# A later place for woven products, and two output weights that stay, in a two-layer streaming encoder

## The chip, the cores and the metric

The program runs on one core of one Trainium2 chip. The metric is device time in microseconds of one execution. TensorE multiplies, VectorE, ScalarE and GpSimd do the rest, and SyncE (SP) issues nearly all DMAs. Each engine works through its own instruction list in order: an instruction that waits holds up all behind it on that engine.

## What is computed

One step of a small encoder for 1024 prompt frames and 32 sample frames (1056 columns), model width 1024, all in float32. Layer 0 is an mLSTM mixer (8 heads, chunks of 64 frames, a recurrence from chunk to chunk), layer 1 a sliding-window attention of 16 query heads over two shared key/value heads. A SwiGLU feed-forward (width 2816) follows each, and every part ends in a LayerNorm of `alpha * x + part(x)`.

```
x = layer_norm(ALPHA * x + mix, ln_g[layer, 0], ln_b[layer, 0])
x = layer_norm(ALPHA * x + swiglu(x, w_gu[layer], w_down[layer]), ln_g[layer, 1], ln_b[layer, 1])
```

For layer 1, `mix` is `o.reshape(B, T, D_ATT) @ w_out`, with `o` the attention's output; this last product with `w_out` (in the kernel `wout_b`) is one of the two places of the change.

## The kernel before

**Products.** Every large product is made of three float32r matmuls per 128 rows (high times high, high times low, low times high: lines 677, 678, 679 in `gemm`). Columns are cut in three groups of 384, 384 and 288 for projections, and in four quarters of 264 for output tiles, LayerNorms and the feed-forward. An output tile (`out_tile`) is 24 matmuls: 8 row blocks of a weight times 3, and a weight comes in two halves of 512 KB each (`f` 0 and 1), the split float32r form that is stored in DRAM after its first use (`wout_b<-w`, `wout_b<-area`) and loaded again later (`w<-wout_b`, line 425).

**Weights.** `Weights` runs a fixed list of units, each with two halves as jobs. A half takes one of five buffers `w` (SLOTS) until `W.done`, or a place of its own (`W.home`) where one is set. Raw weights (`wr<-in_gu` and the like) come by line 372.

**Weaving.** The main program writes out the weight products; small tasks (mLSTM chunks, attention, LayerNorms) are generators that say with `At(engine, reads, ...)` what they wait for next. A planner in the kernel (`Clock`) keeps due times of all tiles while the program is written. After each three matmuls of `gemm`, `Weave.tick` takes tasks whose step is due by `now + LEAD`; `now` is the planner's TensorE time, and for TensorE's steps LEAD is -0.2 us, so they are written only when their operands are due 0.2 us ago or earlier. `Weave.until` and `drain` step the earliest task whatever its due time, with no lead, until a condition holds; the main program uses them where it needs a result.

**mLSTM (70 to 302 us).** Each of 36 chunk items has on TensorE: the score product L1216, the key transpose L1218, the value products L1239 and L1241, the state product L1243, and at last the transposes L1305 of the result `ht`, with VectorE, ScalarE and GpSimd work between.

**Attention (1200 to 1447 us).** 72 items, each of two score products (L2049, L2050) per head, softmax work, transposes L2068 into a tile `T`, a cast to `hi` (L2074, ScalarE) and a subtraction to `lo` (L2078, VectorE), then the value products L2084 (`hi`) and L2085 (`lo`) into `O`. Beside them a list PLAN of weight products runs: queries, and output tiles ("o") of quarters 0 and 1; their weights are loaded for each. At the end the attention's result is copied to SX pieces (L2117, L2119), and act is read back (L2121).

**Late quarters.** After PLAN a `Mixer` opens the area E (`ex`), and `norm_tail` runs quarters 0 to 3: for 0 and 1 the tiles are done, `late_out` only notes them; for 2 and 3 it computes 8 output tiles, m = 0 to 7. `U_OUT_B` are eight units loaded anew for this: the first two take `w` buffers, the other six have homes in E (the first half of tile 2 still takes a buffer). Each quarter's LayerNorm is a woven task: mean and variance products (L737) on TensorE, additions L921, squares L757, folds L744, and so on to SX pieces (L794, L800), which the feed-forward's products then read. The LayerNorm of a quarter starts after that of two quarters before. The first block of the feed-forward (`up_plain`) runs on two quarters, and waits for all LayerNorms before its second half.

Of the kernel before, what the change touches and what calls it, by code (L numbers as in the profile page):

```python
# [19 lines left out]
KT = D // P  # L20
# [264 lines left out]
class Weave:  # L285


    LEAD = {"PE": -0.2}

    def __init__(self, clk):  # L290
        self.clk, self.tasks = clk, []
# [12 lines left out]
    def tick(self, until=0.0):  # L304
        while True:
            now = max(self.clk.now, until)
            best = None
            for i, t in enumerate(self.tasks):
                at = self._start(t)
                if at is not None and at <= now + self.LEAD.get(self._engine(t), 0.45):  # L310
                    if best is None or at < best[0]:
# [204 lines left out]
def kernel(ctx: ExitStack, tc: tile.TileContext, A, O):  # L516
# [41 lines left out]
    def add(name, idx):  # L558
        units.append(A[name][idx] if idx is not None else A[name])
        return len(units) - 1  # L560
# [19 lines left out]
    def again(name, m):  # L580

        u = add(name, m)
        if (name, m) in split:
            halves[u] = split[name, m]
        else:
            split[name, m] = kept[u] = dram.tile([P, 2, 2, D // 2], F32, name=f"{name}_{m}")
            first[name, m] = u
        return u

    def add_ffn(layer):  # L590
        up, dn = {}, []
        for c in range(2):
            for i in range(FIRST):
                up[i, c] = [add("gu", 2 * (layer * FT + i) + k) for k in range(2)]
        for i in range(FIRST, FT):
            up[i] = add_pair("gu", 2 * (layer * FT + i))
        for b in range(TAIL):
            dn.append([add_pair("dn", 4 * (layer * TAIL + b) + 2 * j) for j in range(2)])
        dn.append([add("dnt", KT * layer + m) for m in range(KT)])
        on_vector.update((u, 1) for u in dn[TAIL])  # L600
        on_vector.update((u, 1) for i in range(FIRST) for c in range(2) for u in up[i, c])
        U_UP.append(up)
        U_DN.append(dn)
# [15 lines left out]
    U_B = {}  # L619
    for kind, m, g in PLAN:  # L620
        name, m0 = {"q": ("wqb", m), "k": ("wkv", 0), "v": ("wkv", 1), "o": ("wout_b", m)}[kind]
        U_B[kind, m, g] = again(name, m0)
    U_OUT_B = [again("wout_b", u) for u in range(8)]
    add_ffn(1)
    on_vector.update((u, 1) for u in U_OUT_A)
    on_vector.update((u, f) for u in U_Q[:1] + U_KV + [U_B['q', 0, 0]] for f in range(2))
# [5 lines left out]
    W = Weights(nc, clk, new_weight, units, pairs, on_vector, kept, halves, wv)  # L632
# [824 lines left out]
    lx = Mixer(ea.close, U_OUT_A[:6])  # L1457
# [19 lines left out]
    def out_tile(u, m, g, hold=False):  # L1477
        cols = group(g)
        t = psbank(hold)
        ps, z = t[:, :N4], ACT[:, m, cols]  # L1480
        gemm(ps, wcols(u), [(SX[:, 0, k, cols], SX[:, 1, k, cols]) for k in range(KT)])

        def out():
            yield At("DVE", [ps], [z])
            nc.vector.scalar_tensor_tensor(z, z, ALPHA, ps, op0=ALU.mult, op1=ALU.add)
            release(psx[1][0], "d", t)

        if hold:
            return wv.launch(out(), True)
        nc.vector.scalar_tensor_tensor(z, z, ALPHA, ps, op0=ALU.mult, op1=ALU.add)  # L1490
# [396 lines left out]
    eb = ExitStack()  # L1887
# [10 lines left out]
    def k_part(src, c0, n):  # L1898

        for g in range(2):  # L1900
            r = slice(64 * g, 64 * g + 64)
            o = slice(64 - 64 * g, 128 - 64 * g)
            dst = slice(c0, c0 + n)
            nc.scalar.copy(KH[g][r, dst], src[r])
            nc.vector.tensor_sub(KL[g][r, dst], src[r], KH[g][r, dst].bitcast(F32))
            nc.scalar.copy(KH[g][o, dst], KH[g][r, dst].bitcast(F32))
            nc.vector.tensor_copy(KL[g][o, dst], KL[g][r, dst].bitcast(F32))
# [16 lines left out]
    def q_group(j, g):  # L1924

        t0, n = GRP[g]
        t, ps = project(U_B["q", j, g], g, True)
        W.done(U_B["q", j, g])
        sc = -(HD ** -0.5)

        def out():
            yield At("Activation", [ps], room=[ring(pb, "Q", 4)])
            q = Q[j, g] = new(pb, "Q", [P, 2, 384], F32R, bufs=4)
            for h in range(2):
                r = slice(HD * h, HD * h + HD)
                nc.scalar.activation(q[r, h, :n], ps[r], AF.Copy, scale=sc)
            for h in range(2):
                r, o = slice(HD * h, HD * h + HD), slice(HD - HD * h, P - HD * h)
                yield At("DVE", [q[r, h, :n]])
                nc.vector.scalar_tensor_tensor(  # L1940
                    q[o, h, :n], ps[r], sc, q[r, h, :n].bitcast(F32), op0=ALU.mult, op1=ALU.subtract
                )
            release(psx[1][0], "d", t)
            ast["ready"] += 1

        wv.launch(out(), True)
# [7 lines left out]
    def v_parts(c, src, L):  # L1954

        src = src.rearrange("p (g d) -> p g d", g=2)
        nc.scalar.copy(VR[:L, c, :, 0, :], src)
        nc.vector.tensor_sub(VR[:L, c, :, 1, :], src, VR[:L, c, :, 0, :].bitcast(F32))
# [41 lines left out]
    def v_turn(group):  # L2000
        for c, c0, L, g, off in CH:
            if g == group:
                yield At("PE", [vT[g][:, off : off + L]], room=[ring(psb, "O", 2)])
                pt = new(psb, "O", [P, 512], bufs=2, hold=True)
                nc.tensor.transpose(pt[:L, :P], vT[g][:, off : off + L], ident[:])
                yield At("Activation", [pt[:L, :P]])
                src = pt[:L, :P].rearrange("p (g d) -> p g d", g=2)
                nc.scalar.copy(VR[:L, c, :, 0, :], src)
                yield At("DVE", [VR[:L, c, :, 0, :]])
                nc.vector.tensor_sub(VR[:L, c, :, 1, :], src, VR[:L, c, :, 0, :].bitcast(F32))  # L2010
                release(psb, "O", pt)
                ast["v"] = c + 1
# [119 lines left out]
    for kind, m, g in PLAN:  # L2132
        u = U_B[kind, m, g]
        if kind == "q":
            wv.until(lambda: ast["scored"] >= 3 * (done - 3))
            q_group(m, g)
            done += 1
        elif kind == "o":
            wv.until(lambda: ast["split"] > g and (not g or ast["scored"] >= min(53 + 3 * m, 72)))
            outs.append(out_tile(u, m, g, True))  # L2140
            W.done(u)
        else:
            for t in (1, 2):
                (k_group if kind == "k" else v_group)(u, t)
                if kind == "v":
                    wv.launch(v_turn(t))
            W.done(u)
            if kind == "v":
                v_parts(9, cv[:], P)
                k_part(ck, SEQ, P)  # L2150
                nc.sync.dma_start(O["p_k"], kout[:, :P])
                nc.sync.dma_start(O["s_k"], kout[:, P:])
                nc.sync.dma_start(O["p_v"], vT[2][:, 128:256])
                nc.sync.dma_start(O["s_v"], vT[2][:, 256:])
    wv.drain(task)
    wv.drain(parts)
    for t in outs:
        wv.drain(t)
    lx = Mixer(eb.close, U_OUT_B[2:])

    def late_out(g, cols, after):
        for m in range(KT):
            if g > 1:
                out_tile(U_OUT_B[m], m, g)
                if g == 3:
                    W.done(U_OUT_B[m])
            after(range(KT), m)

    tasks = norm_tail(2, late_out, [lx])
    ffn(1, 3, tasks, lx, True)  # L2170
    wv.until(lambda: not wv.tasks)
# [126 lines left out]
```

## Time and profile before

| | us |
|---|---|
| median of 3 runs | 2220.59 (2217.61 to 2221.95) |
| the profiled execution | 2219.07 |
| its span in the trace | 2217.3 |
| TensorE busy (matmul) | 2182.8 |
| VectorE, ScalarE, GpSimd busy | 1512.6, 1021.9, 800.0 |

Lines are those of the code above. A "wait" of an engine is idle time just before an instruction, with the instruction that released it; a row of the timeline has it in brackets. The chain of waits goes back from the last instruction to what released each step. T in names is a PSUM tile, `d` the PSUM tile of a weight product, `ln` that of a LayerNorm's product.

### The profile page before, as it was taken

The page shows a single profiled execution, that of the slowest core. Times are in us where ns is not written, and L with a number is a line of the kernel's source. Part 1 is how long each engine was busy: PE and PEld are TensorE (multiplying, and loading weights), DVE is VectorE, ACT ScalarE, POOL GpSimd, SP SyncE. Part 2 cuts the span into 40 slices and gives each one's busy share as a digit, 9 for nine tenths or more (in the row PEclk, how much of TensorE's full clock was granted, in tenths as well). Part 3 has the DMA queues.
Part 4 walks back from the last instruction along what each step waited for, and adds up shares of the span by engine and source line. Part 5 has one row for each costly group of instructions (what it writes and reads, how often), then busy time and mean ns, then how long its engine had stood idle before and what let it go on. Part 6 is the DMA issues. An engine that isn't in the chain of part 4 may idle for free.

```text
span 2217.3 us, 44432 instructions
## 1 busy us (share of the span) xinstructions
PE 2182.8 (98%) x17116; PEld 2150.9 (97%) x17116; DVE 1512.6 (68%) x3030; ACT 1021.9 (46%) x2308; POOL 800.0 (36%) x805
## 2 busy tenths in 40 slices
PE   9999999999999999999999999999999999999997
PEld 9989999999999999999999999989999999999997
DVE  5566566777766566476677887778675665566677
ACT  4554454555434444321245877657443443421234
POOL 1343300001544545444401565500454554544510
PEclk9999999999999999999999999999999999999999
DMA  4455522302434424598516568761344344489712
GB/s 154 143 155 174 185 81 74 118 30 77 170 123 173 148 107 165 188 309 283 174 66 223 175 194 267 233 212 58 117 166 146 128 155 145 135 290 322 244 52 78
DMA packets 218052, 356.69 MB, mean 161 GB/s; under 512 B 18608, under 2 KB 151016, under 8 KB 217840
## 3 DMA queue, kind: packets, MB, share of 16 engines
q1 hardware_dynamic: 212800, 348.54, 47.0%
q10 hardware_dynamic: 5040, 5.31, 0.7%
q8 instruction: 135, 2.21, 0.4%
q14 instruction: 77, 0.63, 0.1%
HBM read 251.96 MB, written 101.82 MB: 160 GB/s over the span
## 4 chain that ended last, share of the span: by engine, by line
PE 85%; DVE 5%; DMA 4%; ACT 3%; issue 1%; SPq 1%; POOL 1%; ACTq 0%; DVEq 0%; POOLq 0%
PE d L677 10%; PE d L678 10%; PE d L679 10%; PE A L677 9%; PE A L679 9%; PE A L678 9%; PE B L677 7%; PE B L678 7%; PE B L679 7%; PE T L2068 1%; PE O L2085 1%; PE psS L2049 1%; PE O L2084 1%; PE psS L2050 1%; DMA wr<-in_dn 1%
## 5 line engine op out<-in xcount | busy, mean ns | idle before, releaser
L443 POOL TENSOR_TENSOR w<-wr,w 128x512 fp32r<-128x512 f32 x395 | 561.5, 1437 | 796.2 <-ACT w L429 793.5
L429 ACT CAST w<-wr 128x512 fp32r<-128x512 f32 (+1 forms) x478 | 290.3, 617 | 454.6 <-DVE wr L390 262.7
L677 PE MATMUL A<-sx,w 128*128 128x264 f32 x1280 | 364.1, 284 | 4.2 <-ACT z L1706 3.7
L679 PE MATMUL A<-sx,w 128*128 128x264 f32 x1280 | 363.4, 284 | 0.0
L678 PE MATMUL A<-sx,w 128*128 128x264 f32 x1280 | 363.1, 284 | 0.0
L677 PE MATMUL d<-sx,w 128*128 128x264 f32 (+2 forms) x1092 | 339.5, 311 | 3.3 <-DMA w<-wout_b 2.8
L678 PE MATMUL d<-sx,w 128*128 128x264 f32 (+2 forms) x1092 | 329.5, 302 | 1.5 <-DVE sx L800 1.5
L679 PE MATMUL d<-sx,w 128*128 128x264 f32 (+2 forms) x1092 | 329.3, 302 | 0.0
L677 PEld LDWEIGHTS A<-sx,w 128*128 128x128 f32 x1280 | 240.4, 188 | 5.1 <-ACT z L1706 4.1
L679 PEld LDWEIGHTS A<-sx,w 128*128 128x128 f32 x1280 | 241.2, 188 | 0.0
L678 PEld LDWEIGHTS A<-sx,w 128*128 128x128 f32 x1280 | 240.8, 188 | 0.0
L677 PE MATMUL B<-ex,w 128*128 128x264 f32 x832 | 236.6, 284 | 0.0
L679 PE MATMUL B<-ex,w 128*128 128x264 f32 x832 | 235.9, 284 | 0.0
L678 PE MATMUL B<-ex,w 128*128 128x264 f32 x832 | 235.9, 284 | 0.0
L677 PEld LDWEIGHTS d<-sx,w 128*128 128x128 f32 x1092 | 205.5, 188 | 5.3 <-DMA w<-wout_b 3.0
L678 PEld LDWEIGHTS d<-sx,w 128*128 128x128 f32 x1092 | 205.8, 188 | 2.6 <-DVE sx L800 2.1
L679 PEld LDWEIGHTS d<-sx,w 128*128 128x128 f32 x1092 | 205.4, 188 | 0.0
L677 PE MATMUL d<-sx,ex 128*128 128x264 f32 x552 | 160.3, 290 | 0.0
L1572 DVE TENSOR_TENSOR z<-z 128x528 fp32r<-128x528 f32 x136 | 110.3, 824 | 72.8 <-ACT z L1570 72.5
L679 PE MATMUL d<-sx,ex 128*128 128x264 f32 x552 | 156.7, 284 | 1.1 <-DVE ex L443 1.1
L679 PEld LDWEIGHTS B<-ex,w 128*128 128x128 f32 x832 | 156.8, 188 | 0.0
L678 PE MATMUL d<-sx,ex 128*128 128x264 f32 x552 | 156.7, 284 | 0.0
(303 smaller groups left out, 5858.2 us busy)
## 6 DMA issues: line engine op xcount, KB each, us to landing
wr<-in_gu SPq DMA_DIRECT2D x96, 512.0 KB, 4.8
hs_x<-z SPq DMA_DIRECT2D x72, 528.0 KB, 3.1
hs_t<-z SPq DMA_DIRECT2D x64, 528.0 KB, 3.5
sx<-hs_x SPq DMA_DIRECT2D x112, 264.0 KB, 5.6
w<-wqb SPq DMA_DIRECT2D x48, 512.0 KB, 4.4
sx<-hs_t SPq DMA_DIRECT2D x64, 264.0 KB, 6.0
ex<-hs_t SPq DMA_DIRECT2D x64, 264.0 KB, 6.0
w<-wout_b SPq DMA_DIRECT2D x33, 512.0 KB, 4.3
```

The source lines that it names most:

```text
L429: self.nc.scalar.copy(hi, r)
L443: eng.tensor_sub(lo, r, hi.bitcast(F32))
L677: nc.tensor.matmul(out, ah, bh, start=start and k == 0, stop=False, **kw)
L678: nc.tensor.matmul(out, ah, bl, start=False, stop=False, **kw)
L679: nc.tensor.matmul(out, al, bh, start=False, stop=stop and k == last, **kw)
L1572: clk.sooner(2 * N4, hi).tensor_sub(lo.bitcast(F32R), buf(s), hi)
L2049: nc.tensor.matmul(psS[h][:R, lo:256], q[:, h, tk], KH[g2][:, kc], start=True, stop=False)
L2050: nc.tensor.matmul(psS[h][:R, lo:256], q[:, h, tk], KL[g2][:, kc], start=False, stop=True)
L2068: nc.tensor.transpose(pt[:nk, i, h, :R], p[:R, h, c : c + nk], ident[:R, :R])
L2084: nc.tensor.matmul(po[:, :, :R], v, hi[:nk, i, :, :R], start=(i == 0), stop=False)
L2085: nc.tensor.matmul(po[:, :, :R], v, low[:nk, i, :, :R], start=False, stop=(i == len(kts) - 1))
```

## The change

The lead of woven TensorE steps goes from -0.2 to -0.5 us. The last two output weights of quarter 1 (tiles 6 and 7) aren't given back after it but kept in their four `w` buffers; the late quarters compute the tiles in the order 6, 7, 0 to 5, and the other six weights all have homes in E.

```diff
@@ class Weave
-    LEAD = {"PE": -0.2}
+    LEAD = {"PE": -0.5}
@@ units
-    U_OUT_B = [again("wout_b", u) for u in range(8)]
+    U_OUT_B = [again("wout_b", u) for u in range(6)] + [U_B["o", m, 1] for m in (6, 7)]
@@ PLAN, kind "o"
             outs.append(out_tile(u, m, g, True))
-            W.done(u)
+            if u not in U_OUT_B:
+                W.done(u)
@@ late quarters
-    lx = Mixer(eb.close, U_OUT_B[2:])
+    lx = Mixer(eb.close, U_OUT_B[:6])
 
     def late_out(g, cols, after):
-        for m in range(KT):
+        order = [6, 7, *range(6)]
+        for i, m in enumerate(order):
             if g > 1:
                 out_tile(U_OUT_B[m], m, g)
                 if g == 3:
                     W.done(U_OUT_B[m])
-            after(range(KT), m)
+            after(order, i)
```

What it moves shows at three places. The first is SP's list at the turn to the late quarters; `wout_b_75` to `wout_b_82` are the stored weights of tiles 0 to 7, `act<-scrx` the copies of the last SX step. Before:

```order
L425 DMA w_17769<-wout_b_82 128x2x512
L2121 DMA act<-scrx 128x288
L425 DMA w_17817<-wout_b_82 128x2x512
L425 DMA w_17819<-wout_b_75 128x2x512
L2121 DMA act<-scrx 128x288
L425 DMA w_17894<-wout_b_75 128x2x512
L425 DMA w_17896<-wout_b_76 128x2x512
L2121 DMA act<-scrx 128x288
L425 DMA w_17928<-wout_b_76 128x2x512
L425 DMA w_17930<-wout_b_77 128x2x512
L425 DMA ex_17944<-wout_b_77 128x2x512
```

The same place of the change:

```order
L425 DMA w_17773<-wout_b_82 128x2x512
L2121 DMA act<-scrx 128x288
L425 DMA w_17823<-wout_b_82 128x2x512
L425 DMA w_17825<-wout_b_75 128x2x512
L2121 DMA act<-scrx 128x288 x3
L425 DMA ex_17946<-wout_b_75 128x2x512
L425 DMA ex_17946<-wout_b_76 128x2x512 x2
L425 DMA ex_17946<-wout_b_77 128x2x512 x2
```

Four loads into `w` between the copies are gone (the second half of tile 0, both halves of tile 1, the first of tile 2); these now go to `ex` behind the copies. The four loads of tiles 6 and 7 into `ex`, further down, are gone.

The second is TensorE's list in the mLSTM, around the eleventh `ht` transpose. Before, and then of the change:

```order
L677 MATMUL d_1834<-w_1255,sx 128x256
L678 MATMUL d_1834<-w_1255,sx 128x256
L679 MATMUL d_1834<-w_1255,sx 128x256
L1305 MATMUL T_1914<-ident,ht_1901 128x128 x2
L1239 MATMUL H_1917<-vt_846,p_1869 128x129
L1241 MATMUL H_1917<-Cn_1886,qwz_216 128x129
```

```order
L677 MATMUL d_1928<-w_813,sx 32x256
L678 MATMUL d_1928<-w_813,sx 32x256
L679 MATMUL d_1928<-w_813,sx 32x256
L1305 MATMUL T_1945<-ident,ht_1917 128x128 x2
L677 MATMUL d_1928<-w_818,sx 32x256
L678 MATMUL d_1928<-w_818,sx 32x256
```

The transpose stands some matmuls later, in another weight product, and the value products of the next chunk no longer stand right behind it but ahead of it.

The third is TensorE's list in the attention, at the value products of the 27th item. Its transpose is `T_15557` before, six rows ahead of the first row shown, and its parts are `hi_15570` and `lo_15587`; in the change they are `T_15561`, `hi_15569` and `lo_15574`. Before, and then of the change:

```order
L679 MATMUL d_15531<-sx,w_15417 128x384
L2084 MATMUL O_15577<-hi_15550,VR 128x256
L2085 MATMUL O_15577<-lo_15564,VR 128x256
L2084 MATMUL O_15577<-hi_15550,VR 128x256
L2085 MATMUL O_15577<-lo_15564,VR 128x256
L2068 MATMUL T_15582<-ident,s_15444 128x128 x4
L2049 MATMUL psS_13916<-KH_13918,Q_15332 128x256
L2050 MATMUL psS_13916<-KL_13920,Q_15332 128x256
L2049 MATMUL psS_13917<-KH_13918,Q_15332 128x256
L2050 MATMUL psS_13917<-KL_13920,Q_15332 128x256
L2084 MATMUL O_15603<-hi_15570,VR 128x256
L2085 MATMUL O_15603<-lo_15587,VR 128x256
```

```order
L2084 MATMUL O_15554<-hi_15523,VR 128x256
L2085 MATMUL O_15554<-lo_15548,VR 128x256
L2068 MATMUL T_15561<-ident,s_15426 128x128 x4
L2084 MATMUL O_15578<-hi_15569,VR 128x256
L2085 MATMUL O_15578<-lo_15574,VR 128x256
```

The transpose now stands directly ahead of the products that use its own result; six weight products and nine others no longer lie between.

## Rows read from the trace of the kernel before

**Rows 1.** The page: busy time and instructions of each engine; TensorE's granted clock by slices.

```profile
PE 2182.8 (98%) x17116; PEld 2150.9 (97%) x17116; DVE 1512.6 (68%) x3030; ACT 1021.9 (46%) x2308; POOL 800.0 (36%) x805
...
PEclk9999999999999999999999999999999999999999
```

**Rows 2.** Chain of waits at the program's end: start us, us, what.

```profile
2193.55 0.46 PE ln L737 x2
...
2205.15 0.73 PE ln L882 x2
```

**Rows 3.** Waits of TensorE from 0 to 375 us: us in total, times, longest.

```profile
PE T L1305 <- DVE ht L1299: 2.6, 5, 1.1
...
PE T L1305 <- DVE ks L1225: 0.8, 1, 0.8
PE T L1305 <- DVE Cn L1265: 0.6, 2, 0.3
...
PE S L1216 <- DVE small L1292: 0.5, 1, 0.5
```

**Rows 4.** Timeline of TensorE in the mLSTM: start us, us, line, idle before.

```profile
136.71 0.44 PE L1305 MATMUL T<-ident,ht 128*128 128x128 f32 x2 [1.07 <-DVE ht L1299]
```

**Rows 5.** Stretches: from:to, us, busy us (instructions) by engine, granted clock, DMA, GB/s.

```profile
302.00:364.00 62.00, 62.00 (x390) 61.88 (x389) 37.36 (x76) 29.46 (x61) 0.00 (x0) 1.00 0.11 35
...
700.00:750.00 50.00, 50.00 (x414) 50.00 (x413) 33.75 (x39) 21.72 (x41) 25.14 (x18) 1.00 0.33 120
```

**Rows 6.** Waits of TensorE from 1130 to 1447 us.

```profile
PE O L2085 <- DVE lo L2078: 1.0, 2, 0.8
PE psS L2049 <- DVE st L2100: 0.4, 1, 0.4
```

**Rows 7.** Timeline of all engines in the attention.

```profile
1272.55 0.60 PE L2068 MATMUL T<-ident,s 128*128 128x128 f32 x4
...
1276.68 0.39 PE L2085 MATMUL O<-lo,VR 128*128 128x256 f32 x1 [0.80 <-DVE lo L2078]
...
1288.22 0.60 PE L2068 MATMUL T<-ident,s 128*128 128x128 f32 x4
...
1289.48 0.69 DVE L2078 TENSOR_TENSOR lo<-T,hi 128x512 fp32r<-128x512 f32 x1
```

**Rows 8.** Timeline of all engines at the turn to the late quarters.

```profile
1448.33 0.43 DVE L1485 SCALAR_TENSOR_TENSOR act<-act,d 128x264 f32<-128x264 f32 x1 [1.24 <-PE d L679]
...
1452.11 0.43 DVE L744 TENSOR_TENSOR z<-z 128x264 f32<-128x264 f32 x1
...
1455.41 0.39 PE L677 MATMUL d<-sx,w 128*128 128x264 f32 x1 [2.76 <-DMA w<-wout_b]
...
1455.87 0.39 PE L737 MATMUL ln<-z,onesm 128*128 128x264 f32 x1
```

**Rows 9.** Chain of waits in the late quarters.

```profile
1447.54 7.83 DMA w<-wout_b
...
1533.74 0.72 DVE sx L800
```

**Rows 10.** Waits of TensorE from 1447 to 1545 us.

```profile
PE ln L737 <- DVE z L744: 1.8, 4, 0.7
PE d L678 <- DVE sx L800: 1.5, 3, 1.0
```

**Rows 11.** Timeline at the attention's end: its last value product, its last subtraction.

```profile
1444.17 0.27 PE L2085 MATMUL O<-lo,VR 32*128 32x64 f32 x1
...
1446.63 0.46 DVE L2119 TENSOR_TENSOR sx<-act,sx 128x288 fp32r<-128x288 f32 x1 [0.50 <-ACT sx L2117]
```

**Rows 12.** The page's DMA issues: count, KB each, median us from issue to landing.

```profile
w<-wout_b SPq DMA_DIRECT2D x33, 512.0 KB, 4.3
```

**Rows 13.** Stretches of 2 us at the turn, columns as in rows 5.

```profile
1450.00:1452.00 2.00, 2.00 (x19) 2.00 (x18) 2.00 (x4) 0.00 (x0) 0.00 (x0) 1.00 0.84 192
...
1458.00:1460.00 2.00, 2.00 (x19) 2.00 (x18) 2.00 (x4) 1.69 (x3) 1.34 (x1) 1.00 1.04 393
```

## Prediction

> **What bounds the kernel now.** The page comes first. TensorE is busy 2182.8 us of a span of 2217.3, at a granted clock of nine tenths or more of full speed (2.4 GHz) in all forty slices [rows 1]. The other engines are far from full, so a gain can only come out of the 34.5 us in which TensorE stands still, and 11.4 us of that is the closing chain after its last matmul, from 2205.9 to 2217.3 [rows 2]. The table of waits of TensorE, cut into stretches, then says which of the rest this change can touch. The reader is to see three things in it.
>
> First, between 0 and 375 us eleven waits of woven products (mLSTM) sum to 5.3 us: five of L1305 on `ht` 2.6, one on `ks` 0.8, two on `Cn` 0.6, one of L1216 0.5, and two like it (L1216, L1239) of 0.4 each [rows 3]. The timeline shows one: the transpose of L1305 sits 1.07 us at the head of the queue, and all products behind it sit too [rows 4]. After that, from 302 to 364 us, TensorE is busy 62.00 of 62.00 us [rows 5]: what is saved before is not eaten there.
>
> Second, in the attention (1130 to 1447 us) the waits sum to 1.6 us, two rows and one more of 0.2 [rows 6]. The longest, 0.8 at 1276.68, is in a stretch where `until` forces the chain and few weight products lie between its products [rows 7].
>
> Third, at the turn to the late quarters one wait of 2.76 us on `w<-wout_b` [rows 8]. That load was issued at 1447.54 and took 7.83 us [rows 9]. The mean product of the first LayerNorm (L737, 1455.87) stands three matmuls behind this wait, and the chain of waits runs from it through VectorE and ScalarE to the SX pieces of the last quarter at 1533.74, for which TensorE waits again, 1.5 us [rows 8 to 10]. So the wait sets the end of this stage, both by TensorE's order and by the chain.
>
> **The weights of tiles 6 and 7.** The change removes four loads and lets the late quarters begin with 48 matmuls on resident weights. A matmul of 264 columns costs 0.12 us (414 in 50 us) [rows 5]. Call T the end of the last tile of quarter 1, about 1448.2 in the trace (the addition L1485 that it releases begins at 1448.33; 36 matmuls follow before the wait) [rows 8]. Before, the late load (tile 1, second half) is needed at T+4.4 and lands at T+7.2. After, the first load into `ex` is needed at T + 48 x 0.12 + two L737 at 0.25 + 12 x 0.12 = T+7.7. It can be issued when the attention has left the pool and the last parts are copied: the last attention product ends 24 matmuls before T, that is T-2.9; from there to the end of the last subtraction L2119 took 2.65 us before (1444.44 to 1447.09) [rows 11], and SP has a short copy or so left (estimate 0.4 us), so T+0.2. The window is 7.5 us. A `w<-wout_b` load takes 4.3 us in the median and took 7.83 here [rows 9, 12]; in the new order only copies of 144 KB are ahead of it, in the old one two weight loads were. Behind it ten more loads of `ex` and three raw ones of `in_gu` share the engines: at the 393 GB/s of this stretch [rows 13] 0.524 MB takes 1.33 us, thirteen take 17.3 us, while TensorE needs the last one 10 x 1.45 + 0.5 = 15.0 us after the first. So the first must be 2.3 us early. With 4.3 us it is 3.2 early and nothing waits: gain 2.8. With 7.83 it is 0.3 late, the last 2.6 late: gain 0.2. I take **2.0**, nearer to the median row since less stands ahead. The LayerNorm follows: the operand of its first mean product is ready at T+4.3 (end of L744) [rows 8], and the new order has the product 42 matmuls after T, at T+5.1, so nothing new is late there; the old one came at T+7.7. The order in which tile results are added (6, 7, 0 to 5) costs nothing, since each sum still waits for the eighth tile. That the two weights hold four of five slots until quarter 3 costs nothing: before, tiles 0, 1 and half of 2 held all five. One more output weight is prepared in the mLSTM's shadow; I cost that at nothing, as ScalarE and VectorE have room there; if the cover were gone, it would be two casts of 0.62 us.
>
> The Trainium skill, page "DMA: Bandwidth & Descriptors", section "Specifications", speaks against this: it limits one core to about 358 GB/s from HBM. By it a load takes 1.46 us and the thirteen 19.0, so even after a median first load the last would be 0.8 us late, and the rival of full gain below would give 2214.3 in place of 2213.5. The rows disagree: 393 GB/s in this very stretch [rows 13].
>
> **The later placement.** A woven product is put into TensorE's order when the planner takes its operands to be due 0.5 us ago, not 0.2; the planner looks after each three weight products (0.36 us), so a product moves by none or one such step, 0.3 us on average. A wait shrinks by 0.3 us if the planner's error stays what it was. Eleven waits of 0.3 or more in the mLSTM give 11 x 0.3 = 3.3 us. Bounds: 5.3 if all go; a loss of 1.1, the longest wait of a row, if the new order only brings waits of its own. I take **2.7**, nearer to 3.3, less a little for waits that a new order makes. Behind a waiting transpose stand all weight products, and the next link of the chain; no DMA waits for it alone.
>
> In the attention the forced steps ask no lead, so the five waits there don't shrink by rule; they move. In the new order one transpose L2068 stands directly ahead of the products of L2084 and L2085 that use its own result. From the transpose to the end of the `lo` subtraction it takes 1.95 us where nothing disturbs (1288.22 to 1290.17) and 4.1 where ScalarE and VectorE are crowded (1272.55 to 1276.68) [rows 7]. The transposes and the first product cover 0.55, so the new wait is 1.4 to 3.6 us, against 1.6 that may go: between 0.2 gained and 2.0 lost. I take a loss of **0.5**, nearer to the undisturbed row.
>
> At the end, the variance product of the third quarter (L737, 2193.55 in the chain) has no wait of its own; it stands behind matmuls, and the chain runs from it to the end of the program [rows 2]. It moves behind three more matmuls: **0.3** lost, between 0 and 0.36. The other LayerNorm products wait 1.8 us in the late quarters [rows 10]; the same chain sets that stage, so their shorter waits gain nothing.
>
> **The sum** against the profiled run: 2219.07 - 2.0 - 2.7 + 0.5 + 0.3 = 2215.2 us, 3.9 less. The profiled run lies 1.5 below the median 2220.59; taken off the median, 2216.7 us. About 0.2% (4.4 us) is what a measurement of this kernel can tell from no change.
>
> **The rivals.** *Everything asked for goes:* 2.8 + 3.3 + 1.0 (attention waits that the new order loses, with a short new one) = 7.1 less, 2213.5. For it: the mLSTM's waits sit at products that the lead does govern, and eleven of them is a sample that a shift should move. Against: the adjacent pair in the attention. *The loads take the wait's place:* the first `ex` load again needs 7.8 us and the stream behind it is paced by the DMA; gain 0.2 in place of 2.0, sum 2.1 less, 2218.5. For it: between 1450 and 1452 the rate was 192 GB/s with loads queued [rows 13], so this pace has been seen at this place. Against: half a MB less ahead. *Slower:* forced attention steps. Each place where a transpose and its products meet without weight products between costs up to 3.6 us; from three such places on (10.8 against 6.0 of other gain: 2.0 + 2.7 + 1.6 - 0.3) the kernel is 4.8 slower, 2225.4. For it: these steps ignore the lead, so a chain that is put later meets its gate later. Against: the new order shows one such pair. *The change doesn't do what it says:* a lead larger than the planner's error hides nothing more if that error is not in TensorE's clock but in VectorE's queue; then the mLSTM's gain is 0 and the sum 1.2 less, 2219.4.
>
> **How the numbers follow.** Chances: my sum 0.42, everything 0.30, loads 0.12, no effect of the lead 0.08, slower 0.08. Faster by over 0.2% is "everything" and 0.13 of my sum, 0.43; slower is 0.08; the rest, 0.49, is within. The range 2211 to 2222.5 leaves out the slower case, and the far ends of the mLSTM's bounds (5.3 gained, 1.1 lost).
>
> **What would show it.** Right: no TensorE wait on `w` or `ex` after the last tile of quarter 1, L737 following at T+5, 77 us of LayerNorm chain after that as before; waits of L1305, L1216 and L1239 summing to 2 to 3 us; a new wait of L2084 or L2085 of 1.4 us or more where the transpose stands adjacent. Wrong: a wait on `ex<-wout_b` at the third to last tile of quarter 2; mLSTM waits as long as before; TensorE waiting longer on SX pieces (L800) before the second column half of the FFN, which would mean that the chain, not the load, sets that stage.

## The result: slower, and the time is lost in the attention

The changed kernel takes 2229.12 us (median of 6 runs, 2227.06 to 2233.87) against 2220.18 of the kernel before (6 runs, 2217.61 to 2221.95): a ratio of 1.0044 [1.0031, 1.0057], some 9 us slower. Forecast were 2216.7 us and a range from 2211 to 2222.5. The profiled execution took 2227.06 us; the page shows its span, and TensorE busy 1.0 us longer than in [rows 1], at a granted clock that again reads 9 in every slice (a slice is some 55 us long, and a fall of a few us doesn't show in it):

```profile
span 2225.2 us, 44443 instructions
...
PE 2183.8 (98%) x17116; PEld 2152.0 (97%) x17116; DVE 1511.5 (68%) x3040; ACT 1023.7 (46%) x2310; POOL 789.5 (35%) x797
...
PEclk9999999999999999999999999999999999999999
```

**Where it went.** The weight products (L677 to L679) come in the same sequence in both kernels, 15600 of them, so the k-th starts so much later or earlier in one trace than in the other. This lag of after against the profiled run of before is +0.9 us when the mLSTM and its projections are over (386 us), +1.2 ahead of the attention (1178), **+10.8** when the attention is over, +7.6 when the late quarters have begun, and +7.5 at the end. So the attention lost 9.65 us, the turn won 3.2, and the mLSTM, which should have won 2.7, lost a little.

The stretch from the weight product that starts the attention to the one that ends it, in the view by stretches (from:to, us, busy us with instruction counts of TensorE, weight load, VectorE, ScalarE, GpSimd, then granted clock, DMA, GB/s). The kernel after the change:

```profile
1179.02:1461.84 282.82, 274.29 (x2023) 268.52 (x2022) 211.33 (x739) 196.13 (x579) 136.28 (x184) 0.99 0.65 209
```

The kernel before, in a second execution that was traced later (e8 below; the first has the same 273.17 us and 271.49 busy):

```profile
1176.72:1449.90 273.18, 271.49 (x2024) 266.79 (x2023) 212.40 (x743) 195.07 (x578) 134.31 (x182) 1.00 0.69 221
```

TensorE stands still 8.5 us in place of 1.7, and is busy 2.8 us longer for the same work. Its waits there, of after (us in total, times, longest), answer to [rows 6]:

```profile
PE psS L2049 <- DVE st L2100: 2.5, 4, 1.7
PE d L677 <- DMA w<-wout_b: 2.5, 1, 2.5
PE O L2085 <- DVE lo L2078: 1.8, 2, 1.0
PE d L677 <- PE d L679: 0.9, 1, 0.9
PE O L2084 <- ACT hi L2074: 0.7, 1, 0.7
```

The longest score wait is at 1279.01. The chain of waits of after tells what stood ahead of it on VectorE (start us, us, what):

```profile
1275.63 0.60 DVE lo L2078
1276.23 0.46 DVE sx L2119
...
1276.73 0.55 DVE Q L1940
...
1277.30 0.56 DVE Q L1940
...
1277.87 0.28 DVE act L2093
...
1278.46 0.17 DVE st L2060
1278.63 0.32 DVE s L2100
...
1279.01 0.39 PE psS L2049
```

The score product needs the reduction L2100 of an earlier one, and that is queued behind 3 us of other VectorE work. TensorE had nothing else: its list has no weight product between the products of the items here. At once the granted clock falls, by stretches of 2 us of after:

```profile
1278.00:1280.00 2.00, 0.99 (x5) 0.99 (x6) 1.65 (x9) 0.98 (x3) 1.18 (x3) 0.92 0.38 134
1280.00:1282.00 2.00, 2.00 (x10) 2.00 (x10) 1.79 (x9) 2.00 (x9) 2.00 (x5) 0.50 0.25 77
1282.00:1284.00 2.00, 2.00 (x13) 2.00 (x12) 0.45 (x3) 0.60 (x3) 2.00 (x3) 0.73 0.16 54
```

0.50 is the lower of the two levels, 1.2 in place of 2.4 GHz; TensorE works on at half speed, which costs 1.7 us (each stretch's length times what is missing to 1.00, summed). That is the larger part of the 2.8 us of extra busy time; where the other 1.1 us come from was not traced. The second cluster holds the adjacent pair of the prediction (timeline of TensorE):

```profile
1305.73 0.39 PE L2085 MATMUL O<-lo,VR 128*128 128x256 f32 x1 [1.04 <-DVE lo L2078]
...
1306.19 0.60 PE L2068 MATMUL T<-ident,s 128*128 128x128 f32 x4
1307.47 0.38 PE L2084 MATMUL O<-hi,VR 128*128 128x256 f32 x1 [0.68 <-ACT hi L2074]
1308.57 0.39 PE L2085 MATMUL O<-lo,VR 128*128 128x256 f32 x1 [0.72 <-DVE lo L2078]
```

And near the end of the attention a weight of quarter 1 is late, at 1448.49, by 2.5 us. Its load, in the chain of waits of after:

```profile
1441.63 6.82 DMA w<-wout_b
```

It took 6.82 us, where the median of such loads before is 4.3 [rows 12]; with 4.3 it would have landed at 1445.9, in time. Directly ahead of it in SP's list stand three copies `act<-scrx`, for which SP waited 2.4 us on L2119.

### The profile page after: what moved, and what is told of

It reads as the page before. It is cut to its first block, busy times and chain, and to the rows that moved or that the text cites. A ratio compares the mean times of both kernels' runs of the same rounds, so it can differ in the third digit from the quotient of the medians.

```text
span 2225.2 us, 44443 instructions
## 1 busy us (share of the span) xinstructions
PE 2183.8 (98%) x17116; PEld 2152.0 (97%) x17116; DVE 1511.5 (68%) x3040; ACT 1023.7 (46%) x2310; POOL 789.5 (35%) x797
## 4 chain that ended last, share of the span: by engine, by line
PE 85%; DVE 5%; DMA 4%; ACT 3%; issue 1%; POOL 1%; SPq 0%; ACTq 0%; DVEq 0%; POOLq 0%
PE d L677 11%; PE d L678 10%; PE d L679 10%; PE A L677 9%; PE A L679 9%; PE A L678 9%; PE B L677 7%; PE B L678 7%; PE B L679 7%; PE T L2068 1%; ACT act L787 1%; PE O L2084 1%; PE psS L2049 1%; DMA wr<-in_dn 1%; PE O L2085 1%
## 5 line engine op out<-in xcount | busy, mean ns | idle before, releaser
L443 POOL TENSOR_TENSOR w<-wr,w 128x512 fp32r<-128x512 f32 (+1 forms) x394 | 561.5, 1441 | 937.9 <-ACT w L429 924.5
L677 PE MATMUL A<-sx,w 128*128 128x264 f32 x1280 | 364.6, 285 | 4.6 <-ACT z L1706 3.9
L679 PE MATMUL A<-sx,w 128*128 128x264 f32 x1280 | 363.7, 284 | 0.0
L677 PE MATMUL d<-sx,w 128*128 128x264 f32 (+2 forms) x1092 | 339.6, 311 | 3.9 <-DMA w<-wout_b 2.5
L679 PE MATMUL d<-sx,w 128*128 128x264 f32 (+2 forms) x1092 | 329.7, 302 | 0.0
L677 PEld LDWEIGHTS A<-sx,w 128*128 128x128 f32 x1280 | 241.0, 188 | 5.4 <-ACT z L1706 4.3
L679 PEld LDWEIGHTS A<-sx,w 128*128 128x128 f32 x1280 | 241.6, 189 | 0.0
L677 PE MATMUL B<-ex,w 128*128 128x264 f32 x832 | 236.6, 284 | 0.0
L679 PE MATMUL B<-ex,w 128*128 128x264 f32 x832 | 235.9, 284 | 0.0
L677 PEld LDWEIGHTS d<-sx,w 128*128 128x128 f32 x1092 | 205.7, 188 | 6.4 <-DMA w<-wout_b 2.7
L679 PEld LDWEIGHTS d<-sx,w 128*128 128x128 f32 x1092 | 205.6, 188 | 0.0
L677 PE MATMUL d<-sx,ex 128*128 128x264 f32 x552 | 160.7, 291 | 0.0
L679 PE MATMUL d<-sx,ex 128*128 128x264 f32 x552 | 156.7, 284 | 1.1 <-DVE ex L443 1.1
L679 PEld LDWEIGHTS B<-ex,w 128*128 128x128 f32 x832 | 156.8, 189 | 0.0
```

The source lines that it names most:

```text
L443: eng.tensor_sub(lo, r, hi.bitcast(F32))
L677: nc.tensor.matmul(out, ah, bh, start=start and k == 0, stop=False, **kw)
L679: nc.tensor.matmul(out, al, bh, start=False, stop=stop and k == last, **kw)
```

## The experiments

All start from the changed kernel unless said otherwise. The waits, lags and stretches come from one trace each, the ratios (to the kernel before, run beside them) from all runs.

A count that is used below: ahead of some products of PLAN stands an `until`; for a query product it is `ast["scored"] >= 3 * (done - 3)`, since its result takes the Q buffer that the items scored before have to leave. Where this doesn't hold yet, `until` writes out the steps of small tasks that are still missing, at once, with no weight product between. Counted while the program is written, the kernel before has 22 such **forced steps** at two query products, the changed one 85 at four. An output product has an `until` of its own, and a weight product one for its PSUM tile; forced steps that are left when the query product's condition is moved stand at these.

### The two parts apart, and the kernel before once more

e1 keeps the weights and goes back with the lead; e2 is the kernel before with the new lead; e8 is the kernel before.

```diff
 e1, on the changed kernel
-    LEAD = {"PE": -0.5}
+    LEAD = {"PE": -0.2}
 e2, on the kernel before
-    LEAD = {"PE": -0.2}
+    LEAD = {"PE": -0.5}
```

> The two output weights stay, the lead is -0.2 as before. TensorE's list of instructions then is that of before in the mLSTM and the attention. If the two parts of the change simply add: the attention takes what it took before, the 2.76 us wait at the turn is gone, gain of 2 to 3 us in the lag of the weight products after it, 2217.3 us (ratio 0.9987). Rival, the loads' own cost (one more output weight prepared early, four buffers held): the lag of about 1 us seen at 320 us in the changed kernel, or the new 2.5 us wait on a weight of quarter 1 at 1448.5, shows here too, and the time is 2220 or more.

> The lead is -0.5, the output weights are loaded as before. TensorE's list of instructions in the mLSTM and the attention is that of the changed kernel. If the lead alone makes the loss: about 1 us lost in the mLSTM, 9 to 10 us in the attention, the old wait on the weight at the turn is back, 2231 us or more (ratio 1.005). Rival, the loss in the attention comes from the weights (loads that collide): the attention takes what it took before, 2221 us.

> The kernel before once more, for a second trace of the same list of instructions. If the 2.76 us wait on the weight at the turn is a fixed price, it is here again within 0.5 us. If it hangs on how long that load takes in one execution (7.83 us there, 4.3 in the median), it is 0 to 2 us here, and that is why the weights alone gained nothing that could be measured. The mLSTM's lag against the first trace tells the scatter of that stage: 0 to 1 us expected.

e1: 2218.93 us, ratio 1.0001 [0.9993, 1.0010]. e2: 2228.86 us, 1.0049 [1.0037, 1.0061]. So the lead alone makes the loss: the attention of e2, whose list on TensorE there is that of the changed kernel, takes 284.4 us, with waits at the same places. The weights alone gain nothing that can be measured, though e1's trace shows the 3.0 us at the turn. e8 tells why, and that e2 doesn't have the old wait back, as was expected. The same load for which TensorE waited 2.76 us in [rows 8], in e8's timeline:

```profile
1451.70 0.39 PE L677 MATMUL d<-sx,w 128*128 128x264 f32 x1 [0.19 <-DMA w<-wout_b]
```

With 0.4 for the first `ex` load, 0.6 us in all. The load was issued at 1446.40, so it took about 5.3 us and not 7.83. In e2, where the weights are loaded too, the lag at the turn also falls by 2.65 us against the first trace of before. The 2.76 us belonged to one execution. (e8's profiled run took 2216.02 us, 3.1 less than the first, 2.6 of it here.)

### The lead in one stage alone

One line ahead of the attention's tasks: in e3 the lead is -0.5 up to there and -0.2 from there, in e4 the other way round.

```diff
 e3 (in e4 -0.5, with -0.2 in the class)
+    wv.LEAD = {"PE": -0.2}
     wv.launch(v_turn(0))
     task = wv.launch(attention())
```

> Weights stay; the lead is -0.5 from the start and -0.2 from the second part of layer 1's attention on (from the first launch of attention tasks). Theory A, a later place is bad in the attention by itself: the attention is as before within 1.5 us, the mLSTM loses the 0.8 us of the changed kernel, 2218 us. Theory B, each new order of the attention has waits of its own and the lead's sign has nothing to do with it: the order of the attention differs here too after its first third (the planner's times have moved), so the attention may lose or win up to 10 us although its lead is that of before, 2212 to 2228.

> Weights stay; the lead is -0.2 up to the attention and -0.5 from there. Theory A (a later place is bad in the attention): loses 8 to 10 us in the attention like the changed kernel, 2226 to 2229 us. Theory B (the loss belongs to one order): the order is another than in the changed kernel, the loss may be anything from -2 to 10 us, 2215 to 2228, and the waits stand at other places than 1208, 1276, 1305 and 1448 us.

e3: 2221.98 us, 1.0012 [1.0003, 1.0020]; attention 275.2 us. e4: 2219.76 us, 1.0007 [0.9998, 1.0015]; attention 275.0 us. So neither part of the lead costs what both cost together, and the lead in the attention is not bad by itself: theory A falls. Both orders of the attention are new ones, with 17 and 91 forced steps and 2.9 and 3.4 us of waits, and no fall of the clock; that is what theory B says, by which each order has waits of its own. But 91 steps that cost 1.8 us also say that the number of forced steps is not a price.

### Moving the condition

e5 and e6 take the `until` away from the query product and put its condition where the result goes into Q; the product itself can go ahead, and holds its PSUM bank from then on. e7 makes the condition stricter by one group, with the old lead.

```diff
 e5 (and e6, with the lead -0.2)
@@ q_group, out()
-            yield At("Activation", [ps], room=[ring(pb, "Q", 4)])
+            i = 8 * g + j
+            yield At(
+                "Activation", [ps], room=[ring(pb, "Q", 4)],
+                when=lambda: ast["made"] == i and ast["scored"] >= 3 * (i - 3),
+            )
+            ast["made"] += 1
@@ PLAN, kind "q"
-            wv.until(lambda: ast["scored"] >= 3 * (done - 3))
 e7, with the lead -0.2
-            wv.until(lambda: ast["scored"] >= 3 * (done - 3))
+            wv.until(lambda: ast["scored"] >= 3 * (done - 2))
```

> The changed kernel (lead -0.5, weights stay), but a query product no longer waits, in the order, until 3 x (done - 3) items have been scored; the same condition stands at the copy of its result into Q. Steps of the attention that such conditions force into the order at once: 85 in the changed kernel (22 in the kernel before), 38 here, all at one place. Theory forced steps (their waits, and what follows from them, make the loss in the attention): waits of TensorE between 1210 and 1320 us fall from 5.0 to 2 to 3 us, the loss in the attention from 9.7 to 2 to 5 us, 2220 to 2224 us. Rival, each step placed 0.3 us later costs by itself, forced or not: 2228 us as the changed kernel.

> The same move of the condition with the lead of before (-0.2) and the weights that stay. Forced steps: 65, at two places, against 22 with the condition where it was. Theory forced steps: slower than the weights alone by 2 to 5 us, 2221 to 2224 us. Rival, the number of forced steps says nothing: 2219 us as with the weights alone.

> Lead -0.2 and the weights that stay; the condition ahead of a query product is one item group stricter, 3 x (done - 2) instead of 3 x (done - 3). Nothing is computed otherwise. Forced steps: 147 instead of 22. Theory forced steps: the loss of the changed kernel without its lead, 8 to 15 us in the attention, 2227 to 2234 us, with waits at six places before 1310 us. Rival, the loss belongs to the lead: 2219 us as with the weights alone.

e5: 2219.95 us, 1.0001 [0.9991, 1.0011]; the attention takes 274.0 us, 8.9 less than in the changed kernel at the same lead and 0.8 more than before, a little better than expected. e7: 2227.92 us, 1.0037 [1.0025, 1.0048], with the old lead; the attention takes 283.0 us. So the loss can be taken away without touching the lead, and made without it. e6 misses: 2219.99 us, 1.0002 [0.9993, 1.0010], 65 forced steps and an attention of 273.7 us, only 0.5 more than before; its forced steps met operands that were ready (1.9 us of waits). The waits of TensorE in e7's attention are nearly all those of the value products for `lo` and `hi`:

```profile
PE O L2085 <- DVE lo L2078: 3.4, 5, 1.1
PE O L2084 <- ACT hi L2074: 2.7, 3, 1.6
PE psS L2049 <- DVE st L2100: 0.2, 1, 0.2
```

That is 6.35 us together with short ones, and half speed, which lasts twice as long here as in after, costs 3.4 us. Two of e7's stretches:

```profile
1270.00:1272.00 2.00, 1.35 (x5) 0.82 (x5) 2.00 (x5) 0.82 (x3) 0.00 (x0) 0.78 0.39 101
...
1274.00:1276.00 2.00, 2.00 (x9) 2.00 (x8) 1.02 (x5) 1.20 (x4) 1.61 (x3) 0.50 0.58 129
```

### Other leads, with the condition in either place

e9 and e10 are e5 with the leads -0.45 and 0.0, chosen since no step is forced then; e11 and e12 are e1 with 0.0 and -0.35.

```diff
 e9
-    LEAD = {"PE": -0.5}
+    LEAD = {"PE": -0.45}
```

> Condition at the copy into Q as in the experiment with the later gate, weights stay, lead -0.45: no step of the attention is forced into the order any more. Theory (waits come from forced steps): the attention loses less than before's 1.7 us of waits, at most 1 us; the mLSTM takes 0 to 3 us more than in the first trace of before, as all of them do; 2216 to 2219 us. Rival, a later place costs by itself: 2221 or more.

> The same with lead 0.0, no step forced either. Theory: as with -0.45 in the attention, 2216 to 2219 us; since woven products of the mLSTM are placed 0.2 us sooner than before, a wait there may grow by 0.2 us each, eleven of them, so up to 2.2 us more, 2221. If the lead matters in the mLSTM as the prediction had it (0.3 us for 0.3 us of lead and wait), this kernel is 4 to 5 us slower than the one with -0.45 (11 x 0.45).

> Condition ahead of the query product as before, weights stay, lead 0.0: 17 forced steps (22 with -0.2). Theory forced steps: no loss in the attention beyond 1 us, 2218 to 2221 us.

> Condition ahead of the query product as before, weights stay, lead -0.35, nearer to before's than the change's -0.5: 122 forced steps at eight places. Theory forced steps: a loss like the changed kernel's or more, 2226 to 2233 us. Rival, the loss grows with the lead: half of the changed kernel's, 2222 to 2224 us.

e9: 2214.64 us, 0.9973 [0.9963, 0.9983], faster than both kernels and than expected. e10: 2224.99 us, 1.0020 [1.0011, 1.0029], where 2221 at most, or 4 to 5 us above e9, was expected; it is 10.4 us above e9. e11: 2229.99 us, 1.0039 [1.0025, 1.0054], where 2218 to 2221 was expected. e12: 2227.04 us, 1.0030 [1.0021, 1.0040], as expected; but in this order layer 1 computes something else in part (where was not found), so its time is only a guide, and no conclusion below rests on it.

e10 and e11 lose most of it where the attention has no part in it: they are 6.9 and 6.4 us late at 386 us. The three largest waits of e11 up to 375 us are the mLSTM's:

```profile
PE T L1305 <- DVE Cn L1265: 2.1, 5, 0.9
PE T L1243 <- DVE ks L1225: 2.1, 2, 1.4
PE T L1218 <- DVE act L1310: 1.9, 3, 1.2
```

In the attention, e10 with no forced step takes 272.2 us; e11, with 17 at one place, 276.2: 2.0 us of waits and a fall of the clock of 1.7. So few forced steps can cost much, and the count failed as a price a third time.

### One difference at a time

e13 is e9 with the condition where it was (77 forced steps), e14 is e9 with the eight weights loaded anew (and with the late quarters' order and homes of before, not shown below), e15 is e9 with the lead -0.25 (15 forced steps), e16 is e9 again.

```diff
 e14, on e9
-    U_OUT_B = [again("wout_b", u) for u in range(6)] + [U_B["o", m, 1] for m in (6, 7)]
+    U_OUT_B = [again("wout_b", u) for u in range(8)]
...
-            if u not in U_OUT_B:
-                W.done(u)
+            W.done(u)
...
```

> Lead -0.45, weights stay, condition ahead of the query products as before: 77 forced steps at five places. Against e16 only the condition's place differs. Theory forced steps: 5 to 12 us slower than e16 (2214.6 when it ran as e9), 2220 to 2227 us, all of it between 1210 and 1460 us. Rival, the lead -0.45 happens to be good: 2215 to 2217 us here too.

> As e16 (lead -0.45, condition at the copy into Q), with the output weights loaded anew as in the kernel before. Against e16 only the weights differ. If the gain of the weights is what three traces with loads suggest (the wait at the turn was 2.76 in one, 0.6 and 0.9 us in two), this is 0.5 to 3 us slower, 2215 to 2218 us.

> Condition at the copy into Q, weights stay, lead -0.25: 15 forced steps at one place. Theory forced steps: the attention within 1 us of before's, 2216 to 2220 us. If each order is a lot of its own: anything from 2214 to 2226.

> The kernel of e9 once more beside the three others: 2214 to 2217 us, no wait of TensorE in the attention over 0.5 us but the one of 0.9 at its start.

e13: 2219.42 us, 0.9994 [0.9985, 1.0002]. e16: 2213.67 us, 0.9968 [0.9956, 0.9980]. They differ in the condition's place alone, by 5.7 us of time; and the attention takes 276.86 us in e13 and 271.11 in e16, 5.75 less. e13 and then e16, by stretches:

```profile
1178.26:1455.12 276.86, 272.71 (x2024) 268.39 (x2022) 210.42 (x740) 196.05 (x579) 134.81 (x183) 0.99 0.65 211
```

```profile
1176.72:1447.83 271.11, 270.19 (x2023) 266.92 (x2022) 210.72 (x741) 195.90 (x579) 135.12 (x182) 1.00 0.67 218
```

TensorE stands still 4.15 us in the one and 0.92 in the other, and the clock, which fell in e13 after a wait of 2.7 us of L2049, takes 1.7 more. The waits of e16 in the attention are two:

```profile
PE d L677 <- PE d L679: 0.9, 1, 0.9
PE ln L737 <- DVE z L744: 0.4, 1, 0.4
```

(The second is already beyond the attention's end.) e15: 2218.63 us, 0.9987 [0.9978, 0.9997], attention 271.5 us. e14: 2220.01 us, 0.9995 [0.9986, 1.0003], 6.3 us above e16 and more than was expected of the weights. Of the 6.3 us of lag between the two traces 3.6 arose before 386 us, where both have the same list on every engine: TensorE waits 1.95 us more in e14, and behind its wait of 1.9 us on L1305 at 152 us the clock falls, which costs 1.7. In the attention, again with one list, e14 loses 0.9 more. In the late quarters, where the lists differ, it loses 2.0: the lag at the turn falls by 3.1 us in it and by 3.2 in e16, but by 1545 us e14 has lost 1.7 of that again, with a wait of 2.0 us on an SX piece (L800) where e16 has 1.1, and e16 has won 0.3 more. Why the medians of 12 and 5 runs are as far apart as these two traces was not found.

The attentions of the kernels that have one lead throughout, side by side (length; waits; loss by the clock, in us; forced steps in brackets; e12 is left out):

| lead | condition ahead of the product | condition at the copy into Q |
|---|---|---|
| 0.0 | e11: 276.2; 2.0; 1.7 (17 forced) | e10: 272.2; 0.2; 0 (none) |
| -0.2 | before, e8, e1: 273.1 to 273.2; 1.7; 0 (22) | e6: 273.7; 1.9; 0 (65) |
| -0.25 | | e15: 271.5; 0.7; 0 (15) |
| -0.45 | e13: 276.9; 4.2; 1.7 (77) | e9, e16: 271.1; 0.9; 0 and e14: 272.0; 1.2; 0 (none) |
| -0.5 | after: 282.8; 8.5; 1.7 and e2: 284.4; 10.0; 1.7 (85) | e5: 274.0; 2.7; 0 (38) |

The lengths follow the last two numbers to within 2.5 us: the same work, plus TensorE's waits, plus the half clock. At three of four leads the moved condition wins 4 to 10 us; at -0.2 it wins nothing, since that order had found only 1.7 us of waits. Five orders with the moved condition take 271.1 to 274.0 us, six with the condition ahead of the product (e3 and e4 among them) 273.1 to 284.4. That the moved condition only drew luckier orders is thus unlikely, but with so few orders not excluded.

## Why the prediction was wrong

**What bounds the kernel, and the sign of each place** were read rightly: TensorE is the bound, and what TensorE waits sets the time. The sum failed in its third term, the attention; the mLSTM and the weights were mis-sized.

**The attention: 0.5 us of loss forecast, 9.65 measured.** This is the step that failed. The prediction looked in the new order for a transpose directly ahead of its own products, found one, and priced that: 1.4 to 3.6. The pair did cost 0.68 + 0.72 = 1.4 us. But what is written out without weight products between is set by `until`, and its four places in the new order were not counted: 85 forced steps in place of 22. The waits in and about them are 5.0 us (the L2049, L2085 and L2084 rows above), of which the longest, 1.7, stood behind VectorE's queue and not behind a transpose. The 1.6 us that "may go" ([rows 6] make them four waits, not five) are within these 5.0. To that come 2.5 us for a late weight near 1448, which both executions of this order have (3.2 us in e2, where the load took 7.53) and no other order by over 0.3, 0.9 at the attention's start, which the orders with -0.45 or -0.5 up to there have, and 1.7 by the clock. In sum: waits of 8.5 less the 1.7 of before, and 2.8 us of longer busy time, of which 1.7 by the clock, make the 9.6 us. The clock had no term in the prediction at all. Whether that weight is late for its place behind the copies in SP's list or for its slow load was not tried.

**The rival "slower: forced attention steps"** named the right place, and had a chance of 0.08. Its price was not what happened: it wanted three places or more where a transpose stands directly ahead of its products, at up to 3.6 us each, and there was one such pair, of 1.4; that its 2225.4 us come near 2229.1 is luck. What spoke against it, one pair in the order, was the wrong count. What is now shown: moving the condition takes the loss away at an unchanged lead (e5; e13 against e16), and tightening it makes the loss at the old lead (e7). What is not shown is a price per forced step: e4 and e6 had many that cost little, e11 few that cost 3 us. In the traces they cost where their operands come late through VectorE's or ScalarE's queue.

**The mLSTM: 2.7 us of gain forecast, none found.** The waits sum to 6.2 us in place of 5.3 [rows 3]; those for `ht` nearly went, and others came:

```profile
PE T L1305 <- DVE Cn L1265: 2.9, 3, 1.8
PE T L1218 <- DVE act L1310: 1.4, 3, 0.6
PE H L1239 <- DVE p L1221: 1.0, 1, 1.0
...
PE S L1216 <- DVE p L1221: 0.6, 1, 0.6
...
PE T L1305 <- DVE ht L1299: 0.3, 1, 0.3
```

The longest wait here, 1.8, shows that the bound of 1.1 for one new wait was too small. The step that failed here is "a wait shrinks by 0.3 us if the planner's error stays what it was". That a product that comes later delays its own chain, so that the next link waits as long, is the likely reason, but was not tested. (Three of the eleven waits were under 0.3, namely 0.16, 0.19 and 0.25, so even by that rule the gain was 3.0 and not 3.3.) The lag at 386 us, with one list on TensorE at each lead:

| lead | lag at 386 us, in us |
|---|---|
| 0.0 | 6.9, 6.4 |
| -0.2 | 0, 1.1, 1.0, 1.8, 5.0, 4.4 |
| -0.25 | 7.7 |
| -0.45 | 2.4, 3.3, 4.7, 1.1 |
| -0.5 | 0.9, 3.9, 3.8, 4.6 |

Of these, 1.7 us in e3 (the 3.8), e13 (3.3) and e14 (4.7) and 3.4 in e15 (7.7) are the clock, which fell between 150 and 170 us behind waits of woven products. No lead below 0.0 stands out from a scatter of 5 us that the prediction, made from one trace, could not see. That 0.0 is some 4 us worse than -0.2 is likely, but rests on two traces, and the one trace at -0.25 is as late.

**The weights: 2.0 us of gain forecast.** In the trace it is 3.2, beyond the upper bound of 2.8, with no wait on `w` or `ex` after the last tile of quarter 1 and L737 at T + 5 (1464.02, T being about 1459.0), as forecast. In the runs it is nothing that can be measured (e1 against before; after, 1.0044, against e2, 1.0049); the 6.3 us between e14 and e16 lie for the larger part where the weights don't act. The term set the new order's load at the median of 4.3 us, and the old order's at the 7.83 of the one execution. With 4.3 there too, issued at T - 0.7 and needed at T + 4.4, the old load is in time, and there is no wait to remove. In e8 it took about 5.3 us, and the wait was 0.19.

**The end: 0.3 us of loss forecast, none found.** The lag stays at 7.5 us from 2126 us to the last weight product. Behind it the closing chain took 0.5 us longer than in the first trace of before, but in e1, with the old lead, it took 0.9 longer, so this is no loss that could be put down to L737.

## What to carry to other kernels

Where a planner writes an engine's list, count what a condition forces into it at one place, before and after, and put such a condition at the last point that needs it (here the copy into Q, not the product before it): that was worth 5.7 us at one lead. The fastest version (0.9973 and 0.9968; beside it only e15 is below the kernel before, by 0.1%) needed that, the kept weights and the lead -0.45 together: with any one of the three undone (e13, e14, e15) 5.0 to 6.3 us go again. The condition's share is the attention's; the other two arose in the traces for the most part in the mLSTM, where the scatter is nearly as large. A placement constant that is moved by a little makes a new order everywhere behind it, so its effect has to be measured at several values, and its price can't be read from the waits of the old order. A wait that one trace shows on a DMA is a gain only if it is there with that transfer's usual duration.

## What the runs showed of the hardware

**Half speed after waits.** The granted clock fell to 0.50 (1.2 GHz) in the midst of the kernel after waits of TensorE, and each fall cost 1.7 us beside the wait (3.4 in e7 and in e15). The longest wait just ahead of a fall was between 0.7 us (e3, at 167 us) and 3.2 us (e2, at 1449). It is no fixed function of the list: in e2, with the same list as after, the clock stayed at 1.00 through the same place at 1280 us and fell after the late weight instead:

```profile
1280.00:1282.00 2.00, 2.00 (x17) 2.00 (x16) 1.62 (x8) 1.98 (x9) 2.00 (x4) 1.00 0.06 9
...
1450.00:1452.00 2.00, 2.00 (x11) 2.00 (x10) 0.34 (x1) 0.92 (x2) 0.00 (x0) 0.50 0.95 360
```

The first trace of before has such a fall too, at 950 us behind a wait of 2.57 us, and so has after, behind 2.65 (the same wait took 1.70 us in e8, and the clock stayed).

**The same load, the same place, two times.** 512 KB that were waited for 2.76 us in one execution cost 0.19 us of wait in another; the rate in the stretch from 1450 to 1452 us was 192 GB/s in the first [rows 13], 258 in the second, which is 1.1 us ahead there.

**The scatter sits in some stages.** With one list, the mLSTM's end came up to 5.0 us apart from trace to trace, with no fall of the clock in it, while the attention took 273.17, 273.18 and 273.11 us in three.
